# A two-layer decoder trunk: the third strip of each feed-forward part takes four of its eight pairs of row tiles in seven products

## The chip, the cores and the metric

The kernel runs on one core of a Trainium2 chip. The metric is the device time of one launch in microseconds (us). TensorE (PE) multiplies, with its weight loads shown as PEld; VectorE (DVE) and ScalarE (ACT) do the elementwise work; GpSimd (POOL) and SyncE (SP) mainly start transfers.

## The reference, cut to what matters

```python
def swiglu(x, w_gate, w_up, w_down):
    return (jax.nn.silu(x @ w_gate) * (x @ w_up)) @ w_down

for layer in range(DEPTH):                       # DEPTH = 2
    xn = rms_norm(x, norm_mix[layer])
    x = x + mixer(xn)                            # mLSTM + SSD in layer 0, block attention in layer 1
    x = x + swiglu(rms_norm(x, norm_ffn[layer]), *ffn_params[layer])
return rms_norm(x, final_norm)
```

There are 256 tokens, 2048 features and 5632 hidden columns, all in float32. The weights are float32 too, and each is read from memory once.

## The kernel before, in words

**One product is three multiplications.** Each float32 operand is split into a high part, rounded for TensorE, and a low part, the remainder. A product of two operands is then high x high + high x low + low x high, lines 484 to 486 in `add`, each a matmul of 128x128 by 128x512. The weights are split on the fly: ScalarE casts the loaded tile `raw` to `wh` (line 450) and VectorE subtracts to get `wl` (line 452). `raw`, `wh` and `wl` have three buffers each, and `raw` a fourth, `rawx`, in every fourth turn.

**A strip.** The feed-forward has 11 strips of 512 hidden columns. A strip takes the same 512 columns of the gate and of the up weights and runs through the 16 row tiles of 128 features in 8 steps of two tiles (a pair). With two halves of 128 tokens (t) and two outputs (gate and up) a step is a 2x2 by 2x2 block product. It is done in one of two ways, and `plan` says in which order the two ways come:

- P, an ordinary step: eight products, 24 matmuls, into the four banks of `acc_f`. The elementwise work for it is two casts and two subtractions of 128x1024.
- S, a seven-product step (Strassen's scheme in Winograd's form): 21 matmuls, into `acc_f` and the four banks of `acc_e`. It needs four sums of the weight tiles (`sums`, lines 459, 460 and 462, VectorE), which are cast and split like weights, three weight tiles in one 128x1536 piece, and four sums of the activations (`sf`, lines 315 to 318, split into `skx` or `skh`). These are kept in `kt.sums`, so that later strips take them from there.

`PLAN_X` is `PSPSPSPP`, `PLAN_X4` is `PSPSSPSP`. In both the S steps take the pairs 1, 3, 5 in this order, and in `PLAN_X4` also pair 7. The activations' sums of the pairs 1, 3 and 5 are made when the activations are turned; those of pair 7 are made by `sums_of` (line 326, with `xg` from line 331) at step 3 of the strip that uses them, and lie in `skh`, which has three buffers and is shared with the sums of the hidden activations.

**After the last S step** of a strip the banks `acc_e` are drained: ScalarE copies one (line 530), VectorE adds the others (lines 531, 532 and 535). After the last step VectorE adds `acc_f` to that (line 1067, once for each token half). The next strip's `acc_f` takes the same banks, so its first matmul waits for the first instruction of line 1067. Then come the silu (line 1070, ScalarE) and the product with the up half (line 1071, VectorE), which give `h`. For all but the last strip of a part `h` is copied by a transfer of GpSimd's queue to `hr` (line 1074) and turned by TensorE (line 282) one strip later into the `ha` or `hb` blocks (line 225). It is the end of the held stretch (from the first S step to the last) at which that turning may come.

**A part.** The strips are grouped in parts of 4, 4 and 3. After the strips of a part `add_blocks` multiplies their hidden activations by the down weights, in two blocks of the same kind of steps, with `PSPSPSPP` for parts of four strips and with `PSPSPP` (first block) for parts of three, where the S steps take the pairs 1 and 3. Names: `x1..` and `x3..` are the normed activations of the two layers, `ha` and `hb` the hidden ones, `acc_f`/`acc_e` the accumulators, `pre` the drained sums. In the prediction the strips of a part are counted from one: the third strip is `i == 2`.

**What sets the order.** The program is written step by step; a scheduler then orders each engine's instructions by its own model of time and by the priorities given with `tc.high_priority`. Every engine executes its list in order, so what stands behind a waiting instruction waits too.

The lines around the change are these:

## Time and profile before

| | |
|---|---|
| time, median of 3 runs | 2545.25 us (2544.47 to 2546.2) |
| the profiled execution | 2544.58 us, span 2542.8 us |
| TensorE busy | 2529.4 us, 99% |
| weight loads busy | 2118.3 us, 83% |
| VectorE busy | 2227.9 us, 88% |
| ScalarE busy | 1483.9 us, 58% |

Matmuls are pipelined: the profile gives some 390 ns for one of 128x512, while the next one starts earlier than that, so a busy TensorE says little on how fast it goes. What one costs is read from the distance of starts, and from the length of a stretch with a known count. The same holds for VectorE on a smaller scale: its instructions are shown a little longer than the distance to the next one. The time axis starts with the span. The first feed-forward begins with the strip at 761 us, the second with the one at 1837 us.

### The profile page before, as it was taken

What the parts mean: (1) busy time and instruction counts of PE and PEld (TensorE: products, weight loads), DVE (VectorE), ACT (ScalarE), POOL (GpSimd) and SP (SyncE); (2) the same over time, 40 slices, a digit from 0 to 9 for tenths busy, and PEclk for the clock granted to TensorE, in tenths of its full rate; (3) what the DMA queues carried; (4) which work ended last, traced back from release to release, by engine and by line L of the source; (5) the groups of instructions that cost most, each with busy time, mean ns of one, the idle gap of its engine ahead of it and who ended that gap; (6) DMA issues with size and microseconds to landing.
All of it is one profiled execution on the core that took longest, in us unless ns stands there. A gap on an engine that the chain in (4) does not pass through costs nothing.

```text
span 2542.8 us, 32518 instructions
## 1 busy us (share of the span) xinstructions
PE 2529.4 (99%) x12099; PEld 2118.3 (83%) x12099; DVE 2227.9 (88%) x2839; ACT 1483.9 (58%) x1968; POOL 48.5 (2%) x97
## 2 busy tenths in 40 slices
PE   9999999999999999999999999999999999999998
PEld 8888888888888888888888888888888888888887
DVE  5775788898989999999999986767999999999998
ACT  6465565566656655555455665666565555555564
POOL 1000000000000000000000000000000000000000
PEclk9999999999999999999999999999999999999999
DMA  8565575565565657565666656554556566656664
GB/s 289 174 214 180 170 227 171 177 209 188 191 218 178 224 175 231 192 222 187 218 206 208 198 175 231 165 167 146 199 191 208 200 204 215 214 198 197 227 200 166
DMA packets 256383, 505.40 MB, mean 199 GB/s; under 512 B 15976, under 2 KB 16128, under 8 KB 255712
## 3 DMA queue, kind: packets, MB, share of 16 engines
q1 hardware_dynamic: 249952, 483.20, 58.4%
q0 software_dynamic: 4976, 17.43, 1.8%
q10 hardware_dynamic: 1296, 2.69, 0.3%
q8 instruction: 95, 1.56, 0.2%
q14 instruction: 64, 0.52, 0.1%
HBM read 492.66 MB, written 2.14 MB: 195 GB/s over the span
## 4 chain that ended last, share of the span: by engine, by line
PE 95%; DVE 2%; DMA 1%; issue 1%; ACT 0%; POOL 0%; SPq 0%; POOLq 0%; DVEq 0%; ACTq 0%
PE acc_f L484 18%; PE acc_f L486 18%; PE acc_f L485 18%; PE acc_w L393 11%; PE acc_w L397 6%; PE acc_e L484 4%; PE acc_e L485 4%; PE acc_e L486 4%; PE acc_a L424 2%; PE acc_a L423 2%; PE acc_a L422 2%; PE p_tr L284 1%; DMA raw<-in_l_w_o 1%; PE p_y L919 1%; DVE wl L452 0%
## 5 line engine op out<-in xcount | busy, mean ns | idle before, releaser
L450 ACT CAST wh<-raw 128x1024 fp32r<-128x1024 f32 (+1 forms) x563 | 623.0, 1147 | 387.0 <-PE acc_f L486 313.8
L452 DVE TENSOR_TENSOR wl<-raw,wh 128x1024 fp32r<-128x1024 f32 (+1 forms) x563 | 740.8, 1338 | 84.8 <-ACT wh L450 81.4
L484 PE MATMUL acc_f<-wh,x 128*128 128x512 f32 x1086 | 424.8, 391 | 0.0
L486 PE MATMUL acc_f<-wh,x 128*128 128x512 f32 x1086 | 423.0, 389 | 0.0
L485 PE MATMUL acc_f<-wl,x 128*128 128x512 f32 x1086 | 422.7, 389 | 0.0
L450 ACT CAST wh<-sums 128x1024 fp32r<-128x1024 f32 x250 | 256.6, 1051 | 277.6 <-PE acc_f L486 135.0
L379 DVE TENSOR_TENSOR wl<-raw,wh 128x1024 fp32r<-128x1024 f32 x223 | 269.9, 1222 | 115.7 <-ACT wh L378 113.8
L378 ACT CAST wh<-raw 128x1024 fp32r<-128x1024 f32 x223 | 230.7, 1048 | 183.9 <-PE acc_w L393 94.7
L452 DVE TENSOR_TENSOR wl<-sums,wh 128x1024 fp32r<-128x1024 f32 x250 | 298.5, 1219 | 12.3 <-ACT wh L450 11.8
L393 PE MATMUL acc_w<-xa,wh 128*128 128x512 f32 x768 | 264.6, 395 | 1.2 <-DVE xa L227 1.2
L484 PEld LDWEIGHTS acc_f<-wh,x 128*128 128x128 f32 x1086 | 203.9, 188 | 43.0 <-DVE pre L1067 1.4
L486 PEld LDWEIGHTS acc_f<-wh,x 128*128 128x128 f32 x1086 | 203.9, 188 | 42.6
L485 PEld LDWEIGHTS acc_f<-wl,x 128*128 128x128 f32 x1086 | 203.9, 188 | 41.8
L397 PE MATMUL acc_w<-xa,wl 128*128 128x256 f32 x768 | 208.1, 281 | 0.5 <-DVE wl L379 0.5
L393 PE MATMUL acc_w<-x,wh 128*128 128x512 f32 x512 | 182.2, 399 | 0.0
L393 PEld LDWEIGHTS acc_w<-xa,wh 128*128 128x128 f32 x768 | 143.8, 188 | 31.7 <-ACT wh L371 1.5
L459 DVE TENSOR_TENSOR sums<-raw 128x1024 f32<-128x1024 f32 x125 | 152.4, 1219 | 7.0 <-DMA raw<-in_l_w_out 1.9
L397 PEld LDWEIGHTS acc_w<-xa,wl 128*128 128x128 f32 x768 | 142.0, 189 | 2.1 <-DVE wl L379 0.8
L397 PE MATMUL acc_w<-x,wl 128*128 128x256 f32 x512 | 143.3, 280 | 0.0
L393 PEld LDWEIGHTS acc_w<-x,wh 128*128 128x128 f32 x512 | 96.2, 188 | 20.5 <-DVE rsrc L430 0.4
L484 PE MATMUL acc_e<-wh,skx 128*128 128x512 f32 x261 | 101.7, 391 | 0.0
L486 PE MATMUL acc_e<-wh,skx 128*128 128x512 f32 x261 | 101.6, 389 | 0.0
(364 smaller groups left out, 4678.6 us busy)
## 6 DMA issues: line engine op xcount, KB each, us to landing
raw<-in_l_w_in SPq DMA_DIRECT2D x191, 512.0 KB, 3.8
raw<-in_l_ffn_gate SPq DMA_DIRECT2D x176, 512.0 KB, 4.0
raw<-in_l_ffn_up SPq DMA_DIRECT2D x176, 512.0 KB, 4.9
raw<-in_l_ffn_down SPq DMA_DIRECT2D x176, 512.0 KB, 5.1
raw<-in_l_w_qkv SPq DMA_DIRECT2D x96, 512.0 KB, 4.6
raw<-in_l_w_out SPq DMA_DIRECT2D x64, 512.0 KB, 4.9
raw<-in_l_w_o SPq DMA_DIRECT2D x32, 512.0 KB, 4.7
hr<-h POOLq DMA_DIRECT2D x32, 256.0 KB, 3.2
```

Of the source, the lines that this page charges most:

```text
L378: nc.scalar.copy(wh[:, ks, :], raw[:, ks, :])
L379: turn["low"] = nc.vector.tensor_sub(wl[:, ks, :], raw[:, ks, :], wh[:, ks, :].bitcast(F32))
L393: return nc.tensor.matmul(banks[f], wh[:, kk, f * P:(f + 1) * P], kt.both(k0 + kk), start=k0 + kk == 0, stop=False, skip_group_check=True)
L397: nc.tensor.matmul(banks[f][:, :T], wl[:, kk, f * P:(f + 1) * P], kt.parts(k0 + kk)[0], start=False, stop=k0 + kk == nk - 1, skip_group_ch ...
L422: nc.tensor.matmul(banks[t], xh[:, ts], wh[:, kk, :], start=k0 + kk == 0, stop=False)
L423: nc.tensor.matmul(banks[t], xh[:, ts], wl[:, kk, :], start=False, stop=False)
L450: nc.scalar.copy(h[:, c, :], of[:, c, :])
L452: nc.vector.tensor_sub(l[:, c, :], of[:, c, :], h[:, c, :].bitcast(F32))
L459: nc.vector.tensor_sub(sums[:, 0:2, :], raw[:, 2:4, :], raw[:, 3:0:-2, :])
L484: nc.tensor.matmul(dst, ah, bh, start=start, stop=False)
L485: nc.tensor.matmul(dst, ah, bl, start=False, stop=False)
L486: nc.tensor.matmul(dst, al, bh, start=False, stop=stop)
```

## The change

`PLAN_X4` is now also the plan of the third strip of every part, with the pairs 1, 3, 5 and 7. Only the second strip computes the activations' sums of pair 7; they stay in `kt.sums` for the third.

```diff
         def hidden(hT, i, s, plan, copied):
             more = plan == PLAN_X4
             _, pre, both, joined = block(((wg_, s * STRIP), (wu_, s * STRIP)), xt, 0, KD, plan, pairs=(1, 3, 5, 7) if more else None,
-                                         ahead=((3, sums_of, xt, 7, False),) if more else ())
+                                         ahead=((3, sums_of, xt, 7, False),) if more and i == 1 else ())
...
-                hidden(hT, i, first + i, PLAN_X4 if i == 1 else PLAN_X if first + i else PLAN_LATE, i < n - 1)
+                hidden(hT, i, first + i, PLAN_X4 if i in (1, 2) else PLAN_X if first + i else PLAN_LATE, i < n - 1)
```

Six strips are touched (three parts in each of two layers). In the built program TensorE has 18 matmuls fewer; VectorE has six instructions more of each of the lines 459, 460 and 462, six more `wl` pieces of 128x1536 and twelve more of `wl<-sums`, and twelve fewer of `wl<-raw` of 128x1024; ScalarE has the casts that belong to them. The counts of GpSimd's and SyncE's instructions stay.

**VectorE at the end of the third strip of the first part.** `wl<-raw` of 128x1024 are the weights of ordinary steps, lines 531, 532 and 535 drain `acc_e`, and line 1067 frees the banks that the next strip begins with. Before:

```order
L452 TENSOR_TENSOR wl<-raw,wh 128x1024 x3
L531 TENSOR_TENSOR pre<-pre,acc_e 128x512
L452 TENSOR_TENSOR wl<-raw,wh 128x1024
L532 TENSOR_TENSOR pre<-pre,acc_e 128x512
L452 TENSOR_TENSOR wl<-raw,wh 128x1024
L535 TENSOR_TENSOR pre<-pre,acc_e 128x2x512
L452 TENSOR_TENSOR wl<-raw,wh 128x1024
L459 TENSOR_TENSOR sums<-raw 128x1024
L452 TENSOR_TENSOR wl<-raw,wh 128x1536
L460 TENSOR_TENSOR sums<-raw,sums 128x512
L1067 TENSOR_TENSOR pre<-pre,acc_f 128x1024
```

And with the change, from the last ordinary step's weights on:

```order
L452 TENSOR_TENSOR wl<-raw,wh 128x1024 x2
L1071 SCALAR_TENSOR_TENSOR h<-pre,r_7062,h 128x512
L452 TENSOR_TENSOR wl<-raw,wh 128x1024
L531 TENSOR_TENSOR pre<-pre,acc_e 128x512
L452 TENSOR_TENSOR wl<-raw,wh 128x1024
L532 TENSOR_TENSOR pre<-pre,acc_e 128x512
L459 TENSOR_TENSOR sums<-raw 128x1024
L535 TENSOR_TENSOR pre<-pre,acc_e 128x2x512
L460 TENSOR_TENSOR sums<-raw,sums 128x512
L1067 TENSOR_TENSOR pre<-pre,acc_f 128x1024 x2
```

Before, two ordinary steps follow the last S step, and their weights stand between the drains; now one follows, and the second `h` of the strip before stands in this stretch too.

**TensorE where the fourth strip of the first part begins**, with what it waits for in brackets. `p_tr<-ident_r,hr` turns the hidden activations of the second strip, `x_6962` is the first block of activations. With the change:

```order
L486 MATMUL acc_f<-wh,x_7183 128x512
L282 MATMUL p_tr<-ident_r,hr 128x128 [waits DMASW5_49,DVE_49]
L282 MATMUL p_tr<-ident_r,hr 128x128 [waits DMASW6_49]
L282 MATMUL p_tr<-ident_r,hr 128x128
L282 MATMUL p_tr<-ident_r,hr 128x128 [waits DVE_49,PE_49]
L282 MATMUL p_tr<-ident_r,hr 128x128 x4
L484 MATMUL acc_e<-wh,x_6962 128x512 [waits Activation_49]
L484 MATMUL acc_e<-wh,skx 128x512 [waits Activation_49]
L484 MATMUL acc_f<-wh,x_6962 128x512 [waits DVE_49]
```

The turning now stands behind the third strip's last step, where before that step came behind it, and two matmuls of the fourth strip's first S step stand ahead of its first `acc_f` one.

**VectorE in the first down block of the parts with three strips** (layer 0's is shown). `skh<-sf` is the last piece of the first strip's sums, `ha_11872` the second strip's hidden activations. Before, `skh<-sf` stood in the third strip, ahead of the last S step's weights:

```order
L462 TENSOR_TENSOR sums<-raw,sums 128x512
L1071 SCALAR_TENSOR_TENSOR h<-pre,r_7062,h 128x512
L225 TENSOR_TENSOR skh<-sf,skh 128x4x128
L452 TENSOR_TENSOR wl<-sums,wh 128x1024
L452 TENSOR_TENSOR wl<-raw,wh 128x1024 x3
L531 TENSOR_TENSOR pre<-pre,acc_e 128x512
```

With the change it stands behind the end of the strip:

```order
L1067 TENSOR_TENSOR pre<-pre,acc_f 128x1024 x2
L452 TENSOR_TENSOR wl<-raw,wh 128x1536
L462 TENSOR_TENSOR sums<-raw,sums 128x512
L452 TENSOR_TENSOR wl<-sums,wh 128x1024
L459 TENSOR_TENSOR sums<-raw 128x1024
L452 TENSOR_TENSOR wl<-sums,wh 128x1024
L452 TENSOR_TENSOR wl<-raw,wh 128x1024 x2
L460 TENSOR_TENSOR sums<-raw,sums 128x512
L225 TENSOR_TENSOR skh<-sf,skh 128x4x128
L462 TENSOR_TENSOR sums<-raw,sums 128x512
L225 TENSOR_TENSOR ha_11872<-p_tr,ha_11872 128x2x256
L225 TENSOR_TENSOR ha_11872<-xg,ha_11872 128x2x256
```

Both `skh` and the first `ha_11872` are operands of TensorE in this block: in its list the first `skh` low part comes 38th among the matmuls that follow the wait for line 1067, the first `ha_11872` low part 42nd.

## The prediction

> **What bounds the kernel now.** I read the page first, then who TensorE waits for, then the length of stretches with a known count of matmuls.

> ```profile
> PE 2529.4 (99%) x12099; PEld 2118.3 (83%) x12099; DVE 2227.9 (88%) x2839; ACT 1483.9 (58%) x1968; POOL 48.5 (2%) x97
> PEclk9999999999999999999999999999999999999999
> PE 95%; DVE 2%; DMA 1%; issue 1%; ACT 0%; POOL 0%; SPq 0%; POOLq 0%; DVEq 0%; ACTq 0%
> ```

> TensorE is 95% of the chain that ended last, and its clock is never lowered. VectorE at 88% is close behind. TensorE's waits, listed for the weight loads, are tiny:

> ```profile
> PEld acc_e L484 <- DVE ha L225: 1.6, 6, 0.4
> PEld acc_f L484 <- DVE pre L1067: 1.4, 6, 0.3
> ```

> So six waits for line 1067 cost 1.4 us in the whole run. Next, busy time by stretch: a down block without waits, then the third strip of the first part, the third strip of a three-strip part and the down block behind it (length, TensorE, weight loads, VectorE, ScalarE, GpSimd, clock, transfers):

> ```profile
> 974.32:1015.79 41.47, 41.47 (x184) 34.35 (x183) 37.66 (x36) 21.18 (x20) 0.00 (x0) 1.00 0.63 204
> 847.18:889.39 42.21, 42.21 (x192) 34.87 (x191) 41.76 (x45) 25.24 (x29) 1.08 (x2) 1.00 0.66 226
> 1351.01:1393.23 42.22, 42.22 (x191) 34.86 (x191) 41.76 (x45) 25.24 (x29) 1.07 (x2) 1.00 0.68 225
> 1393.23:1426.04 32.81, 32.81 (x147) 26.53 (x146) 29.52 (x34) 18.50 (x21) 0.00 (x0) 1.00 0.56 179
> ```

> The first row is five ordinary and three seven-product steps, 5 x 24 + 3 x 21 = 183 matmuls, in 41.47 us: one costs 0.2266 us. But in the third strip VectorE is busy 41.76 of 42.21 us, with three seven-product steps. The change puts a fourth one exactly there. TensorE bounds the kernel by a hair, and the question is what VectorE does with more work in a stretch that it already fills.

> **What is saved.** Six third strips lose three matmuls each: 18 x 0.2266 = 4.1 us. This is TensorE's time and lies on the path. It is also nearly all that there is to gain, since the waits above are so small. About 0.2% (5.1 us) is what a measurement of this kernel can tell from no change, so even the whole saving would lie within it.

> **What VectorE pays.** Its costs come from the distance of starts at the end of the second strip, which has the new plan already:

> ```profile
> 837.30 2.36 DVE L452 TENSOR_TENSOR wl<-raw,wh 128x1024 fp32r<-128x1024 f32 x2 [1.18 <-ACT wh L450]
> 839.57 1.22 DVE L459 TENSOR_TENSOR sums<-raw 128x1024 f32<-128x1024 f32 x1
> 840.71 0.68 DVE L531 TENSOR_TENSOR pre<-pre,acc_e 128x512 f32<-128x512 f32 x1
> 841.31 1.22 DVE L452 TENSOR_TENSOR wl<-raw,wh 128x1024 fp32r<-128x1024 f32 x1
> 842.44 0.68 DVE L532 TENSOR_TENSOR pre<-pre,acc_e 128x512 f32<-128x512 f32 x1
> 843.04 1.22 DVE L452 TENSOR_TENSOR wl<-raw,wh 128x1024 fp32r<-128x1024 f32 x1
> 844.18 1.21 DVE L535 TENSOR_TENSOR pre<-pre,acc_e 128x1024 f32<-128x1024 f32 x1
> 845.31 0.68 DVE L460 TENSOR_TENSOR sums<-raw,sums 128x512 f32<-128x512 f32 x1
> 845.91 2.34 DVE L1067 TENSOR_TENSOR pre<-pre,acc_f 128x1024 f32<-128x1024 f32 x2
> ```

> An instruction of 1024 takes 1.14 us to the next start, one of 512 takes 0.60. The third strip gives the other sizes:

> ```profile
> 854.05 2.36 DVE L452 TENSOR_TENSOR wl<-raw,wh 128x1024 fp32r<-128x1024 f32 x2
> 856.33 0.68 DVE L460 TENSOR_TENSOR sums<-raw,sums 128x512 f32<-128x512 f32 x1
> 856.93 1.75 DVE L452 TENSOR_TENSOR wl<-raw,wh 128x1536 fp32r<-128x1536 f32 x1
> 858.60 0.68 DVE L462 TENSOR_TENSOR sums<-raw,sums 128x512 f32<-128x512 f32 x1
> 859.21 0.68 DVE L225 TENSOR_TENSOR ha<-p_tr,ha 128x512 fp32r<-128x512 f32 x1
> 860.40 0.28 DVE L315 TENSOR_TENSOR sf<-xg 128x128 f32<-128x128 f32 x1
> 860.61 0.28 DVE L316 TENSOR_TENSOR sf<-xg 128x128 f32<-128x128 f32 x1
> 861.34 0.75 DVE L1071 SCALAR_TENSOR_TENSOR h<-pre,r,h 128x512 f32<-128x512 f32 x1
> 862.02 2.36 DVE L452 TENSOR_TENSOR wl<-sums,wh 128x1024 fp32r<-128x1024 f32 x2
> 864.29 2.35 DVE L452 TENSOR_TENSOR wl<-raw,wh 128x1024 fp32r<-128x1024 f32 x2
> ```

> That is 1.67 us for 1536, 0.20 for an `sf`, 0.67 for line 1071, 2.27 for two of 1024. A seven-product step costs VectorE 1.14 + 0.60 + 0.60 + 1.67 + 2.27 = 6.28 us while TensorE spends 21 x 0.2266 = 4.76; an ordinary one 2.27 us against 5.44. The change adds 6.28 - 2.27 = 4.0 us of VectorE's work to a strip and takes 0.7 us of TensorE's time away; that the sums of pair 7 are not made again only spares adding more. ScalarE, at 25.24 of 42.21 us, has room.

> **The third strip's end.** With the new order VectorE's list is as before up to 859.21. Behind that I add up, word for word along the list, to the first line 1067. The two seven-product steps in a row come first: line 459 and four pieces of 512 1.14 + 2.40, `sf`, `wl<-sums`, `sf` 2.67, the second step's `wl` 1.67 + 2.27, an ordinary step 2.27, together 12.42. Then the last seven-product step with one line 1071 and two `sf` in it: 1.14 + 1.67 + 0.60 + 1.14 + 0.60 + 1.07 + 1.14 = 7.36. Then the ordinary step's weights 2.27, line 1071 0.67, and the drains with the next weights 1.14 + 0.60 + 1.14 + 0.60 + 1.14 + 1.13 + 0.60 = 6.35. The sum is 29.07 us, so line 1067 starts at 888.28, and at the 1.21 us of line 535's row, which has its size, ends at 889.49. Inside the strip I find the weights ready before TensorE needs them. The closest are the three-tile weights of the second adjoining step: 859.21 + 1.14 + 2.40 + 2.67 + 1.75 = 867.2, wanted after 90 matmuls at 847.18 + 90 x 0.2266 = 867.6. ScalarE's casts come in time by its room.

> When does TensorE come there? The same place at the end of the second strip:

> ```profile
> 846.17 0.80 PE L282 MATMUL p_tr<-ident_r,hr 128*128 128x128 f32 x8
> 846.81 0.46 PE L484 MATMUL acc_e<-wh,x 128*128 128x512 f32 x1
> 847.18 0.50 PE L484 MATMUL acc_f<-wh,x 128*128 128x512 f32 x1
> ```

> Eight turns take 0.64 us; without a wait the `acc_f` matmul would have started at 846.81 + 0.23 = 847.04, so the wait was 0.14. With the change the third strip has 180 matmuls, one of them already done at 847.18: 847.18 + 179 x 0.2266 + 0.64 = 888.38, and two matmuls moved ahead bring 888.83. Line 1067 is seen 0.06 us after its end (847.12 to 847.18), at 889.55: a wait of 0.72 us that the third strip does not have now. Six times that is 4.3 us. Its bounds: 0 if VectorE keeps up after all (no gain, since there is no wait to lose), 2.1 if it loses another 1.4 (the second rival). Behind the waiting matmul the whole next strip is queued, so every bit of it is time; but ScalarE and VectorE get on meanwhile, and the next strip, an ordinary one, lets VectorE recover, so I count nothing there.

> **The three-strip parts.** There the down block follows, and VectorE's late work is an operand. Shifted by 1351.01 - 847.18 = 503.83, line 1067 starts at 1392.11 and TensorE goes on at 1393.38. VectorE reaches the end of the first `ha` piece after 2.26 + 1.67 + 0.60 + 1.14 + 1.14 + 1.14 + 2.27 + 0.60 + 0.60 + 0.60 + 0.68 = 12.70 us, at 1404.81. TensorE wants it after 41 matmuls, at 1393.38 + 9.29 = 1402.67: a wait of 2.2 us, with what it waits for `skh` on the way in it. Later, around the last sums, my adding up finds 0.3 us more. Today's block has a wait of its own: 32.81 - 138 x 0.2266 - about 0.8 for its eight turns = 0.7 us. The difference is 1.7 us, twice in the run 3.4 us. Bounds: - 0.7 (today's wait goes too) to 4 us each, the upper one if the turns of the last strip's `h`, which stand behind, come late too.

> **The sum.** - 4.1 + 4.3 + 3.4 = + 3.6 us on this execution's 2544.58, or 2548.2. It lies 0.67 us below the median of the runs, so the median should come to 2548.8, 0.14% above before: no difference that can be told.

> **The rivals.**

> *The whole saving stays.* The scheduler's model had all these instructions before it, and every wait above is one to two us in a chain of 29 us; if VectorE gains 3% anywhere, the waits shrink to nothing. Then - 4.1 us: 2541.2. For it speaks that the second strip runs with the same plan and 0.14 us of wait; against it that the second strip starts with VectorE well ahead and the third does not.

> *VectorE waits for a load in the two adjoining seven-product steps (slower).* By the adding up above, line 459 wants its load at 859.21. The load into that buffer is issued here, for the up half:

> ```profile
> 854.37 0.47 SPq L443 DMA_DIRECT2D raw<-in_l_ffn_up  x1
> ```

> Now, with another load 2.5 us behind it, these two landed after (shortest, median, longest) the first of these rows, and the four halves of loads at 839 to 846, without one so close, after the second:

> ```profile
> DMA to landing us min/median/max: 5.4/5.8/6.2
> DMA to landing us min/median/max: 3.6/4.0/4.5
> ```

> It lands at 858.9 if alone and at 860.6 if not. With the change the next load waits for a buffer that is free only at 859.2, so it should be alone, with 0.3 us to spare. If it is late by 1.4 us, nothing in the chain takes that up: 6 x 1.4 = 8.4 us more, 2557.2.

> *The copies of h come late.* By the same adding up the third strip's second line 1071 ends at 882.0, and TensorE turns its copy at 887.74. GpSimd's instruction takes 0.54 us, and the copy lands after:

> ```profile
> L1074 POOL DMA_DIRECT2D hr<-h x32: 537/537/603, 811.7 to 2452.6; - x32
> DMA to landing us min/median/max: 2.2/3.2/6.3
> ```

> At the median it is there at 885.7, at the longest at 888.8. Then turns and two matmuls end at 889.9 instead of 888.83, 0.4 us behind line 1067: 6 x 0.4 = 2.4 us more, 2551.2. [...] The trace's spread of 2.2 to 6.3 us fits a hindrance of some kind but does not say which. [...]

> *The sums are not kept.* If the third strip computed pair 7's sums again, VectorE would have 0.60 + 4 x 0.20 + 0.60 = 2.0 us more per strip, 12 us in all, 2560.8; against it, the order has no such instructions.

> **How the numbers follow.** My forecast 0.50, the whole saving 0.15, the late load 0.20, the late copies 0.12, sums not kept 0.03. The forecast's own range, with its waits between half and one and a half, is 2545 to 2553. Slower by over 0.2% (above 2550.3): all of the late load and the last rival, most of the late copies, and about a seventh of the forecast, 0.20 + 0.03 + 0.08 + 0.07 = 0.38. Faster by over 0.2% (below 2540.2) needs the whole saving and another 1 us: 0.04. Within: 0.58. The range leaves out the top half of the late load and a part of the whole saving: 2541.5 to 2556.

> **What would show it.** Right: 18 matmuls fewer, the wait for line 1067 at the starts after third strips at 0.5 to 1 us instead of none, `skh` and `ha` behind line 1067 waited for by TensorE in both three-strip down blocks, some 2 us more there, third strips with VectorE busy throughout. Wrong: third strips shorter by 0.7 us with no wait behind them; VectorE idle on line 459 for a transfer in the two adjoining steps; TensorE waiting for `hr`; or waits anywhere else.

## The result and the profile after

The changed kernel takes 2559.19 us (median of 6 runs, 2557.81 to 2562.59), the kernel before in runs beside it 2544.76 us (6 runs, 2544.29 to 2546.2). The ratio is 1.0058, with a 95% interval of 1.0045 to 1.0071: 14.4 us slower. The forecast was 3.6 us slower, and its range ended at 2556. The profiled execution has a span of 2557.7 us, 14.9 more than before.

The page of the changed kernel, TensorE's clock and the chain that ended last:

```profile
PE 2535.0 (99%) x12081; PEld 2116.2 (83%) x12081; DVE 2250.2 (88%) x2863; ACT 1491.4 (58%) x1974; POOL 49.0 (2%) x97
PEclk9999999999999999999999999999999999999999
PE 84%; DVE 9%; DMA 2%; issue 2%; ACT 1%; SPq 0%; POOL 0%; POOLq 0%; ACTq 0%; DVEq 0%
```

The 18 matmuls are gone. TensorE's share of the chain fell from 95% to 84%, and VectorE's rose from 2% to 9%. The shares of busy time do not show it: they are as before. TensorE's waits, by its weight loads (us in total, times, longest):

```profile
PEld acc_f L486 <- DVE skh L225: 4.3, 2, 2.2
PEld acc_e L484 <- DVE ha L225: 3.8, 6, 1.1
PEld acc_f L484 <- DVE pre L1067: 3.7, 12, 0.6
PEld p_tr L282 <- DMA hr<-h: 3.6, 6, 1.1
PEld acc_e L484 <- DVE hb L225: 2.8, 5, 1.7
PEld acc_e L484 <- ACT wh L450: 2.8, 12, 0.4
PEld p_tr L284 <- DVE h L1071: 2.2, 8, 0.4
...
PEld acc_f L484 <- ACT wh L450: 2.1, 1, 2.1
```

Before, `ha` had 1.6 us, `hb` 1.3 and line 1067 1.4, and the other rows here had at most 0.3 or did not stand in the list. Now these three have 3.8, 2.8 and 3.7 us, and the others come on top. By stretch (length, TensorE, weight loads, VectorE, ScalarE, GpSimd, clock, transfers): two third strips, then the first down blocks of the two three-strip parts:

```profile
846.33:890.01 43.68, 42.40 (x190) 34.49 (x190) 42.51 (x46) 25.97 (x29) 1.07 (x2) 1.00 0.65 218
1353.03:1396.29 43.26, 42.33 (x190) 34.47 (x190) 42.59 (x46) 26.17 (x30) 1.08 (x2) 1.00 0.66 217
1396.29:1432.13 35.84, 34.06 (x144) 27.42 (x145) 33.63 (x38) 18.49 (x22) 0.00 (x0) 0.95 0.52 176
2477.63:2517.51 39.88, 36.38 (x146) 28.54 (x146) 34.07 (x39) 18.15 (x21) 0.00 (x0) 0.91 0.58 186
```

The third strips are longer than before, 43.68 and 43.26 us for 42.2, with fewer matmuls. The block at 1396 takes 35.84 us where it took 32.81, and the last one 39.88 where it took 32.34, as this row of before has it:

```profile
2468.98:2501.32 32.34, 32.34 (x148) 26.61 (x146) 28.86 (x35) 18.07 (x20) 0.00 (x0) 1.00 0.62 197
```

The mean clock of the two blocks is 0.95 and 0.91: the clock was lowered, which the page's slices of 64 us hide.

To see where the time went, I cut the span and compare with the same cuts before (us, profiled executions). A part is counted here from the first `acc_f` matmul of its second strip to the same place of the next part; the first three-strip part ends with its down blocks, the second with the span:

| | four-strip parts (4) | three-strip parts (2, with the end) | the rest |
|---|---|---|---|
| the change | +5.0 | +10.5 | -0.6 |

### The profile page after: what moved, and what is told of

Its sections match the earlier page's. It is cut to its first block, busy times and chain, and to the rows that moved or that the text cites. A ratio compares the mean times of both kernels' runs of the same rounds, so it can differ in the third digit from the quotient of the medians.

```text
span 2557.7 us, 32523 instructions
## 1 busy us (share of the span) xinstructions
PE 2535.0 (99%) x12081; PEld 2116.2 (83%) x12081; DVE 2250.2 (88%) x2863; ACT 1491.4 (58%) x1974; POOL 49.0 (2%) x97
## 4 chain that ended last, share of the span: by engine, by line
PE 84%; DVE 9%; DMA 2%; issue 2%; ACT 1%; SPq 0%; POOL 0%; POOLq 0%; ACTq 0%; DVEq 0%
PE acc_f L484 15%; PE acc_f L486 15%; PE acc_f L485 15%; PE acc_w L393 11%; PE acc_w L397 6%; DVE wl L452 4%; PE acc_e L484 4%; PE acc_e L486 4%; PE acc_e L485 4%; PE acc_a L424 2%; PE acc_a L423 2%; PE acc_a L422 2%; DVE sums L459 1%; ACT wh L450 1%; DMA raw<-in_l_ffn_down 1%
## 5 line engine op out<-in xcount | busy, mean ns | idle before, releaser
L450 ACT CAST wh<-raw 128x1024 fp32r<-128x1024 f32 (+1 forms) x557 | 619.4, 1152 | 342.3 <-PE acc_f L486 279.6
L452 DVE TENSOR_TENSOR wl<-raw,wh 128x1024 fp32r<-128x1024 f32 (+1 forms) x557 | 736.2, 1344 | 75.0 <-ACT wh L450 71.7
L450 ACT CAST wh<-sums 128x1024 fp32r<-128x1024 f32 x262 | 270.1, 1051 | 331.2 <-PE acc_f L486 142.9
L484 PE MATMUL acc_f<-wh,x 128*128 128x512 f32 x1050 | 410.6, 391 | 0.2
L486 PE MATMUL acc_f<-wh,x 128*128 128x512 f32 x1050 | 409.0, 390 | 0.0
L485 PE MATMUL acc_f<-wl,x 128*128 128x512 f32 x1050 | 408.6, 389 | 0.0
L452 DVE TENSOR_TENSOR wl<-sums,wh 128x1024 fp32r<-128x1024 f32 x262 | 313.5, 1219 | 8.6 <-ACT wh L450 7.7
L484 PEld LDWEIGHTS acc_f<-wh,x 128*128 128x128 f32 x1050 | 197.1, 188 | 43.0 <-DVE pre L1067 2.7
L486 PEld LDWEIGHTS acc_f<-wh,x 128*128 128x128 f32 x1050 | 197.1, 188 | 41.1
L485 PEld LDWEIGHTS acc_f<-wl,x 128*128 128x128 f32 x1050 | 197.1, 188 | 40.4
L459 DVE TENSOR_TENSOR sums<-raw 128x1024 f32<-128x1024 f32 x131 | 159.6, 1218 | 10.2 <-DMA raw<-in_l_ffn_down 4.9
L484 PE MATMUL acc_f<-wh,hb 128*128 128x512 f32 (+1 forms) x260 | 101.3, 390 | 1.8 <-ACT wh L450 1.7
L486 PE MATMUL acc_e<-wh,skx 128*128 128x512 f32 x261 | 101.6, 389 | 0.0
```

Of the source, the lines that this page charges most:

```text
L450: nc.scalar.copy(h[:, c, :], of[:, c, :])
L452: nc.vector.tensor_sub(l[:, c, :], of[:, c, :], h[:, c, :].bitcast(F32))
L459: nc.vector.tensor_sub(sums[:, 0:2, :], raw[:, 2:4, :], raw[:, 3:0:-2, :])
L484: nc.tensor.matmul(dst, ah, bh, start=start, stop=False)
L485: nc.tensor.matmul(dst, ah, bl, start=False, stop=False)
L486: nc.tensor.matmul(dst, al, bh, start=False, stop=stop)
```

## The first down block of a three-strip part

VectorE of the changed kernel from line 1067 on (start, us):

```profile
1395.02 2.35 DVE L1067 TENSOR_TENSOR pre<-pre,acc_f 128x1024 f32<-128x1024 f32 x2
1397.28 1.75 DVE L452 TENSOR_TENSOR wl<-raw,wh 128x1536 fp32r<-128x1536 f32 x1
...
1403.15 2.36 DVE L452 TENSOR_TENSOR wl<-raw,wh 128x1024 fp32r<-128x1024 f32 x2
1405.43 0.68 DVE L460 TENSOR_TENSOR sums<-raw,sums 128x512 f32<-128x512 f32 x1
1406.03 0.68 DVE L225 TENSOR_TENSOR skh<-sf,skh 128x512 fp32r<-128x512 f32 x1
1406.63 0.68 DVE L462 TENSOR_TENSOR sums<-raw,sums 128x512 f32<-128x512 f32 x1
1407.24 0.68 DVE L225 TENSOR_TENSOR ha<-p_tr,ha 128x512 fp32r<-128x512 f32 x1
```

From line 1067 to the end of the first `ha` piece are 12.90 us; the adding up in the prediction said 12.70. TensorE at that moment:

```profile
1404.59 0.40 PE L485 MATMUL acc_f<-wl,ha 128*128 128x512 f32 x1
1406.77 0.65 PE L486 MATMUL acc_f<-wh,skh 128*128 128x512 f32 x1 [1.78 <-DVE skh L225]
1407.21 0.63 PE L486 MATMUL acc_e<-wh,skh 128*128 128x512 f32 x1
```

The two starts are 2.18 us apart, and the waits row gives 4.3 us for two of them: the wait of 2.2 us that was forecast. But behind it the next start comes after 0.44 and then 0.43 us, not 0.23. The slow stretches of the changed kernel begin at 1406.96, 2488.99 and 2502.64 us and last 3.41 us each; their beginnings lie 317 and 4 times 3.413 us apart, so I cut the span in steps of that length. The first two rows lie beside this wait, the last two beside the longest wait (1.64 us from start to start) of the four-strip parts (length, TensorE busy, clock, transfers):

```profile
1403.55:1406.96 3.41, 1.63 (x8) 1.00 0.75 220
1406.96:1410.38 3.42, 3.42 (x9) 0.50 1.00 377
2280.77:2284.18 3.41, 2.16 (x10) 1.00 0.01 5
2284.18:2287.60 3.42, 3.42 (x16) 1.00 0.05 10
```

TensorE ran at half its clock for exactly one such stretch after the first wait, and not after the second. It happens three times in the changed kernel, always in three-strip parts, and before not once from 4.69 to 2537.37 us of its span (mean clock 1.00). 19 matmuls took 0.427 instead of 0.227 us, 3.8 us, and those at the stretches' edges were slowed in part (0.40 us at 2488.90). All told it is some 4.8 us: eight matmuls of 0.427 us fill a stretch that would hold fifteen of 0.227, so each of the three cost 1.6 us. In the last part a second wait of 2.1 us follows 13 us behind the first (the row of line 450 with one wait above: the casts are late), with its own slow stretch.

## The experiments

Theory from these rows: VectorE has too much to do, or does it in the wrong order, at the end of the third strip; what the down block needs comes late, and a long enough wait halves the clock. Rivals came with each test. All times are medians, beside the kernel before on the same chip (2544.0 to 2545.4 us). The losses by part, as in the table above, come from each profiled execution. The pieces of code show only what differs, often a part of a line.

| run | time, us | ratio to before, interval | four-strip | three-strip | rest |
|---|---|---|---|---|---|
| e1_four | 2555.31 | 1.0043 (1.0030, 1.0056) | +4.8 | -0.4 | +5.9 |
| e2_three | 2556.56 | 1.0044 (1.0031, 1.0056) | -0.1 | +8.8 | +3.2 |
| e3_prio | 2562.41 | 1.0069 (1.0056, 1.0081) | +4.4 | +12.6 | +1.0 |
| e10_prio2 | 2556.09 | 1.0049 (1.0036, 1.0061) | +6.5 | +5.2 | -0.4 |
| e11_allprio | 2567.90 | 1.0093 (1.0079, 1.0107) | +13.8 | +11.3 | -1.2 |
| e7_less | 2554.58 | 1.0034 (1.0022, 1.0046) | +2.0 | +9.5 | -0.3 |
| e13_less_prio | 2550.14 | 1.0024 (1.0014, 1.0033) | +2.2 | +2.2 | +0.3 |
| e14_double | 2552.59 | 1.0032 (1.0019, 1.0044) | +1.7 | +5.2 | -0.1 |
| e9_pool | 2580.51 | 1.0138 (1.0125, 1.0152) | +19.4 | +17.4 | +1.8 |
| e16_alt | 2557.80 | 1.0053 (1.0039, 1.0067) | +7.0 | -0.1 | +7.4 |
| e6_early | 2587.71 | 1.0170 (1.0156, 1.0184) | +29.1 | +16.7 | -0.7 |
| e4_again | 2599.86 | 1.0219 (1.0203, 1.0235) | +35.2 | +18.0 | +0.3 |
| e5_swap | 2588.63 | 1.0169 (1.0155, 1.0183) | +32.0 | +16.1 | +0.5 |
| e12_fill | 2559.88 | 1.0065 (1.0051, 1.0079) | +9.0 | +8.7 | +0.9 |
| e8_fill | 2585.02 | 1.0155 (1.0141, 1.0169) | +18.4 | +8.9 | +10.1 |
| e15_pad | 2573.75 | 1.0115 (1.0101, 1.0129) | +15.4 | +3.2 | +9.9 |

In the rows quoted from the experiments a line's number can be one to four higher than the change's. Single executions scatter. The four-strip parts have one and the same order in the change, e3_prio, e10_prio2 and e12_fill, and lost 5.0, 4.4, 6.5 and 9.0 us, so a difference of a few microseconds in one column alone says little.

### Which parts lose

e1_four, the new plan in four-strip parts alone; e2_three, with `n == 3`:

```diff
-PLAN_X4 if i in (1, 2) else
+PLAN_X4 if i == 1 or i == 2 and n == 4 else
```

> The new plan for the third strip of the parts with four strips alone (four of the six strips). Theory (the loss sits mainly in the three-strip parts: the down block behind the third strip waits 2 us for the first strip's sums, and TensorE's clock is halved behind that wait): these four parts cost 0.5 to 1.8 us each in the profile of the change, 5.1 us together, so about 2550, and no clock of 0.5 inside the span. Rival (every third strip loses about the same, since VectorE is full in each): two thirds of the 14.4 us, about 2554.

> The new plan for the third strip of the two three-strip parts alone. Theory: these two parts cost 3.8 and 6.7 us in the profile of the change, so about 2555, with the weight-load waits for skh (line 225) of some 2 us each and two or three stretches of 3.4 us at half clock. Rival (every third strip alike): one third of 14.4 us, about 2549.5.

The two add up to 21.8 us, more than the change. By time alone e1_four went to the rival. The time of e2_three is close to the theory's. By part the theory holds for both: each kind loses about what it loses in the change, 4.8 and 8.8 us for 5.0 and 10.5, and the untouched kind nothing. The surplus of e1_four is in "the rest", at the passage from the attention layer to the second feed-forward, where no line differs (of e2_three's 3.2 us 1.6 are lost there). Before, the change and e1_four there:

```profile
1793.33:1881.07 87.74, 87.50 (x403) 72.58 (x402) 84.27 (x109) 56.10 (x79) 0.69 (x1) 1.00 0.62 207
```

```profile
1799.39:1887.14 87.75, 87.46 (x402) 72.57 (x402) 84.12 (x109) 56.70 (x79) 0.69 (x1) 1.00 0.61 206
```

```profile
1795.41:1889.76 94.35, 90.23 (x403) 74.58 (x402) 84.70 (x109) 56.21 (x79) 1.12 (x1) 0.96 0.58 191
```

The same work takes 6.6 us longer. In e1_four the scheduler put two casts of the feed-forward's first weights about 10 us later in ScalarE's list than before, and TensorE waits 3.9 us in one piece:

```profile
PEld p_tr L284 <- ACT skx L225: 3.9, 1, 3.9
```

Behind this wait the clock is at half for 6.83 us (its mean from 1840 to 1850 us is 0.66), which the theory for this run had excluded. So an edit in one place changed the order in another, hundreds of microseconds on. The change itself does not suffer from it (87.75 us).

### The order in VectorE's queue

e3_prio moves the turnings of the three-strip parts forward, e10_prio2 also lines 1070 and 1071 (the silu and the product that make `h`) of their last strip, e11_allprio both in all strips. The lines shown are those of e10_prio2:

```diff
-        with tc.high_priority(offset=1200 if first else 0):
+        with tc.high_priority(offset=1200 if first or kt.name in ("ha8", "hb8") else 0):
...
+                with tc.high_priority(offset=0 if copied or hT.name not in ("ha8", "hb8") else 1200):
```

> The change as it is, but the turning of hidden activations in the three-strip parts is given a higher priority in the scheduler, so that the first strip's sums and the second strip's hidden activations stand earlier in VectorE's list; no work is added or taken away. Theory (late operands and the clock behind them): the waits for skh go, the clock stays full, and 6 to 8 us of the 10.5 us of these two parts come back, 2551 to 2553. Rival (VectorE's total work is the bound there, in whatever order): the waits move to other operands and the time stays within 2 us of 2559.

> As the run that moved the turnings of the three-strip parts forward, and with the two products that make h of their last strip moved forward too (they were what came late there). Theory (it is the order in VectorE's queue: what the down block waits for stands behind splits of weights that are wanted later): the 10.5 us lost in the three-strip parts fall to under 4, no half clock there, 2549 to 2553 us. Rival (VectorE has too much to do at that place whatever comes first, so that another instruction is late by as much): 2556 us or more, with another name in the waits.

> The changed kernel, with the turnings and the products that make h moved forward in all strips of the feed-forward parts. Theory of the order: the waits of the four-strip parts (5 us) shrink as well as those of the three-strip parts, 2541 to 2549 us. Rival (the amount): the splits of weights are late in their place, TensorE waits for wh and wl inside the strips, 2556 to 2575 us.

e3_prio lost no less than the change (more than the rival's bound too), and the theory of the order alone fell. The waits for `skh` left the list; another came:

```profile
PEld p_tr L284 <- DVE h L1071: 8.4, 10, 3.9
```

The turnings now stood ahead of line 1071, TensorE had to wait up to 3.9 us for `h`, and the clock was at half for 6.83 us in each of the two parts (its mean over the execution is 0.996, for 0.997 in the change). With that moved too (e10_prio2) the loss in the three-strip parts is halved, 10.5 to 5.2 us, and no stretch there is at half clock (0.999 over the execution, as before). That is not under 4 as the theory asked, and the time, 2556.1, is at the rival's edge; its interval overlaps that of the change. With everything forward (e11_allprio) the splits of weights are what comes late, as the rival had it:

```profile
PEld acc_e L485 <- DVE wl L452: 21.1, 30, 1.6
PEld acc_e L484 <- ACT wh L450: 11.4, 17, 2.0
```

Whatever is put first, something else is late: the order chooses who waits.

### The amount of VectorE's work

e7_less leaves out three subtractions in the third strip (the sums of weights of its last S step are not formed, and the raw weights are split in their place), e13_less_prio adds e10_prio2's order, e14_double adds three to the kernel before, e9_pool gives three to GpSimd:

```diff
+            if summed == "less":
+                return parts(raw, (slice(0, 3),)) + parts(raw, (slice(0, 2), slice(2, 4)))
...
+            for _ in range(2 if summed == "twice" else 1):
...
+            eng = nc.gpsimd if summed == "pool" else nc.vector
```

> The changed kernel, and for the last of the four seven-product row tiles of the third strip the three VectorE subtractions that build the sums of weights are left out (the raw weights are split in their place), so 1.2 + 0.7 + 0.7 = 2.6 us of VectorE less in each third strip, with the same matmuls. Theory (VectorE's work alone is late): the waits of 2.2 us in the three-strip parts go, and the half clock with them; 2545 to 2549 us. Rival (the waits are set by the order, by the bank that the turning shares or by loads, not by how much VectorE has to do): little changes, 2555 to 2560 us.

> The two partial remedies together: in the third strip the three subtractions for the sums of weights of the last seven-product tile are left out (2.6 us of VectorE; the raw weights are split in their place), and the turnings and the two products for h of the last strip of the three-strip parts are moved forward in the order. Theory (VectorE's amount in the third strip makes the waits, and its order only says which instruction is the late one): with both, the three-strip parts lose under 2 us instead of 10.5, the four-strip parts 1.6 us as with the first alone, no half clock; 2544 to 2548 us. Rival (something besides VectorE, as the banks or the loads, holds the down block): 2551 us or more.

> The kernel before the change, with the three subtractions for the sums of weights of one seven-product tile of the third strip done twice (same values): 2.6 us of VectorE more in each third strip, no matmul moved. Theory (VectorE's work in that strip is what costs): waits appear in TensorE at the same places as with the change, which adds 4.3 us of VectorE: 2547 to 2554 us. Rival (VectorE has slack there, and the fourth seven-product tile hurts through its matmuls, their banks or their place): within 2 us of before.

> The changed kernel, with the three subtractions for the sums of weights of the last seven-product row tile of the third strip on GpSimd instead of VectorE, 2.6 us of VectorE less in each third strip. Theory (VectorE's work is late and GpSimd has time: it is busy 2%): 2545 to 2550 us. Rival (GpSimd takes much longer for them than VectorE's 2.6 us, or slows VectorE while it works, so that TensorE waits for those weights): no better than 2557 us, up to 2580.

e7_less cured the four-strip parts (5.0 to 2.0 us) but hardly the three-strip ones: the time set free was filled with splits for later, and a split became the late one, so that half clock came here too (the first down block of the first three-strip part takes 36.99 us at a mean clock of 0.95). By time, 2554.6 us, it lies at the rival's edge.

```profile
PEld acc_e L487 <- DVE wl L452: 5.2, 6, 2.2
```

With both remedies the loss went from 14.4 to 5.4 us, below the rival's bound but above the theory's 2544 to 2548. The down block of the first three-strip part there:

```profile
1396.15:1429.21 33.06, 33.00 (x146) 26.22 (x146) 31.12 (x36) 18.49 (x22) 0.00 (x0) 1.00 0.62 199
```

33.06 us against 35.84, at full clock, 0.25 us from the 32.81 of before. The other direction, e14_double, is the plainest: no matmul is moved, and 2.6 us of VectorE more in each third strip make the kernel 7.9 us slower, as the theory said. The place is the same, the late operands are not: in the first down blocks of the two three-strip parts TensorE waits for splits (`wl`, 2.0 and 1.3 us) and for `ha` or `hb` (1.0 us each). The clock is 1.00 in the first of these blocks:

```profile
1394.30:1429.52 35.22, 33.35 (x148) 26.39 (x146) 31.57 (x36) 18.70 (x21) 0.00 (x0) 1.00 0.53 174
```

GpSimd is no way out (e9_pool), as the rival had it. Its three pieces take 3.3, 1.6 and 2.7 us, 7.6 together where VectorE takes 2.6, and ScalarE's casts wait for them (20.5 us in six waits). VectorE's pieces are longer there as well: in each of the six strips its split of 128x1536 beside GpSimd's second and third piece took 2.84 or 2.85 us, where others took 1.75; no run shows why.

```profile
L460 POOL TENSOR_TENSOR sums<-raw 128x1024 f32<-128x1024 f32 x6 | 19.8, 3304 | 328.9 <-DMA raw<-in_l_ffn_up 165.2 <-DVE wl L452 163.7
...
L463 POOL TENSOR_TENSOR sums<-raw,sums 128x512 f32<-128x512 f32 x6 | 16.1, 2687 | 0.5
L461 POOL TENSOR_TENSOR sums<-raw,sums 128x512 f32<-128x512 f32 x6 | 9.7, 1619 | 0.5
```

### Its neighbours and its place

e16_alt gives the plan to the second and the fourth strip of four-strip parts, and to the second alone in three-strip parts, e6_early moves its S steps forward, e4_again makes pair 7's sums anew in the third strip, e5_swap has the plan in the third strip alone:

```diff
+PLAN_X4 if i == 1 or i == 3 and n == 4 else
...
+PLAN_X4E = "PSSPSSPP"
...
+ahead=((3, sums_of, xt, 7, False),) if more else ())
...
+PLAN_X4 if i == 2 else
```

> The seven-product strips apart: second and fourth strip in the four-strip parts, only the second in the three-strip parts, with the second strip's sums kept for the fourth. Theory of the amount, with VectorE catching up in the plain strip between: 0 to 0.7 us less in each of the four parts, 2541 to 2546 us. Rival (a seven-product strip straight ahead of a down block costs there, one before it or not): 2 to 3 us more in each of the four parts, 2550 to 2558 us.

> The changed kernel, with the third strip's order PSSPSSPP instead of PSPSSPSP (S: seven products): its last seven-product tile is one tile earlier and two plain ones follow. Theory (what is late is VectorE's drains and turning at the strip's end): the waits of 2.2 us in the three-strip parts shrink below 1 us and the half clock goes, 2548 to 2554 us. Rival (VectorE cannot keep up with seven-product tiles side by side: two pairs of them need 2 x 6.8 us of VectorE for 2 x 4.8 us of TensorE): TensorE waits for weights inside the third strips, 2558 to 2575 us.

> The change, but the third strip computes the activations' sums of pair 7 again (one subtraction pass of 512, four of 128, one split: 2.0 us of VectorE per strip, TensorE the same). Theory: VectorE has no slack between the adjoining seven-product steps and line 1067, so nearly all of it comes on top, 6 x 2.0 = 12 us, 2567 to 2573. Rival (VectorE has slack, only late operands behind the strip count): under 3 us more, 2559 to 2562.

> Only the third strip has four seven-product tiles, the second strip has three as the others; the third strip makes its own sums of activations. As many matmuls as before the change. Theory A (the strip straight ahead of the down block is the wrong place, since VectorE's drains and splits of that strip end late): the three-strip parts keep their loss of 8 to 10 us, the four-strip parts lose nothing against before, 2552 to 2556 us, with waits of 2 us and half clock in the first down block of the three-strip parts. Theory B (two such strips in a row are the trouble, VectorE enters the third strip already behind): one alone costs nothing, 2543 to 2547 us, no wait over 1 us there.

e16_alt went to the rival: with a plain strip between the two, the four parts still lose 7.0 us, 1.8 each, about half of it in the fourth strip and half in the down block behind it. A strip with four S steps straight ahead of a down block costs there. (Another 7.4 us are the passage of e1_four again.) e6_early missed the theory by far, and by another way than its rival's: TensorE waits for the drains of `acc_e`, which the next S step's banks and the turning now need at once.

```profile
PEld acc_e L485 <- ACT pre L531: 13.2, 6, 2.5
PEld p_tr L283 <- DVE pre L532: 7.2, 6, 2.0
```

e4_again and e5_swap were meant as tests of the sums and of the neighbours, and both came out beyond every expectation, so they test neither cleanly. The sums asked for within the third strip come late, by up to 5.3 us in e4_again and 2.9 in e5_swap, and stretches at half clock follow in every part: the mean clock of the two executions is 0.994 and 0.992, for 0.999 before, and in e4_again 0.94 in the 52.78 us of the second part's third strip. First e4_again, then e5_swap:

```profile
PEld acc_f L484 <- ACT skh L225: 29.3, 6, 5.3
```

```profile
PEld acc_f L484 <- ACT skh L225: 14.3, 6, 2.9
```

### The clock, and a tile's place

e12_fill puts eight matmuls by zeros a little ahead of the one that waits for `skh` (the first lines below); e8_fill was the same with a tile of zeros of its own; e15_pad has the kernel before with such a tile, unused:

```diff
+            for _ in range(fill):
+                nc.tensor.matmul(dst[:64], ident_r[0:64, 64:P], bh[0:64], start=False, stop=False)
...
+    none = cst.tile([P, 32], F32, name="none")
+    nc.gpsimd.memset(none, 0.0)
```

> The changed kernel, with eight matmuls by a tile of zeros (they add nothing to the result) put in TensorE's order into the wait of 2.2 us in the first down block of each three-strip part: 8 x 0.227 = 1.8 us. Theory (TensorE waiting for about 2.1 us is what halves the clock): the wait shrinks to some 0.4 us, the half clock after it goes (7 matmuls in the one part, 5 in the other at 0.427 instead of 0.227 us, so 2.4 us), and what follows from the slow stretch in the last part, 2553 to 2557 us. Rival (the clock is lowered for another reason, or the wait is not shortened but the eight come on top): half clock stays, 2559 to 2563 us.

> The changed kernel, with eight matmuls by zeros (a corner of the identity, nothing is added to the result, and no tile is added) in TensorE's order ahead of the matmul that waits 2.2 us in the first down block of each three-strip part: 8 x 0.227 = 1.8 us. Theory (a TensorE idle for about 2 us within one stretch of 3.413 us gets half clock in the next): the wait shrinks to some 0.4 us, no half clock follows it, 12 matmuls at 0.227 instead of 0.427 us or 2.4 us less; the later wait for the casts in the last part may keep its own; 2555 to 2558 us. Rival (the clock goes down for another reason, or the fills come on top): half clock stays at both places, 2559 to 2563 us.

> The kernel before the change, with one unused tile of 128 bytes per partition kept through the kernel, so that all that is placed after it lies 128 bytes further. Theory (the first run with fills took 25 us more than the changed kernel, all of it in matmuls of 232 instead of 227 ns in the strips, because of that tile's place): 2563 to 2573 us. Rival (the zeros themselves did it): 2543 to 2547 us.

In e12_fill every engine has the changed kernel's order but for the 16 fills. While TensorE works on the fills VectorE catches up, and the gap before `skh` is gone in both parts: 0.23 us from start to start instead of 2.18. No half clock follows this matmul: the first part's whole block has 1.00 where it had 0.95. In that part, the fills, the matmul by `skh` with the one ahead of it, and the whole block (as the rows by stretch above):

```profile
1406.78 2.08 PE L487 MATMUL acc_f<-wh,ident_r 64*64 64x512 f32 x8
1410.50 0.39 PE L485 MATMUL acc_f<-wl,ha 128*128 128x512 f32 x1
1410.73 0.39 PE L488 MATMUL acc_f<-wh,skh 128*128 128x512 f32 x1
```

```profile
1399.96:1434.79 34.83, 34.74 (x152) 26.98 (x153) 33.65 (x38) 18.17 (x21) 0.00 (x0) 1.00 0.55 179
```

The block takes 34.83 us instead of 35.84 although 2.0 us of fills are in it. The later gap for casts in the last part is still 2.12 us, so the first slow stretch did not cause it, and it keeps its own half clock (TensorE is busy for 1.66 of the 3.41 us ahead of it, for 1.70 in the change; the mean clock of the execution is 0.998, for 0.999 before). So a wait of this size, 2.18 us from start to start, can lower the clock, as the theory said. The time did not fall as expected and lies in the rival's range: the profiled execution gains 1.8 us in the three-strip parts and loses 4.0 in the four-strip ones, whose order is untouched, and the median is that of the change within the scatter.

e8_fill's 25 us above the change come from the tile's place: e15_pad, without any fill, is 29 us slower than before, a little more than expected. The down block and the strip behind it, the same 183 matmuls each, in e15_pad:

```profile
984.23:1025.72 41.49, 41.49 (x185) 1.00 0.61 203
1025.72:1068.25 42.53, 42.53 (x184) 1.00 0.59 198
```

No wait, full clock, and 1.05 us more in the strip, where before both took 41.48.

## Why the prediction was wrong

**What held.** The saving, 18 matmuls. VectorE's price, 4.0 us a strip (the page has VectorE busy 22.3 us longer, 3.7 a strip), and the adding up along its list: 12.70 against 12.90 us to the first `ha`, and two waits of 2.2 us, as worked out, for what it named. The profiled execution lost 14.9 us where 3.6 were forecast. Of the 11.3 us between, 7.2 lie in the first down blocks of the three-strip parts (10.6 for 3.4) and 3.5 in those of the four-strip parts (3.5 for nothing).

**"Its clock is never lowered."** This was read off the profile before and carried into a program with longer waits. No term of the sum held a clock. It cost some 4.8 us in three slow stretches. Together with the later wait of 2.1 us for casts, which the adding up did not reach, it makes the two blocks, forecast at + 1.7 us each, lose 3.0 and 7.5. This step failed most. In the changed kernel gaps of 2.18, 2.18 and 2.08 us from start to start, in stretches of 3.41 us with TensorE busy for 1.63, 1.64 and 1.70 us, were each followed by 3.41 us at half clock.

**"The next strip, an ordinary one, lets VectorE recover, so I count nothing there."** That strip did not suffer: it is 0.34 us shorter, by the matmuls moved ahead of it. But behind it the first down blocks of the four four-strip parts lost 3.5 us: TensorE's first `acc_e` matmul waits there for `ha` or `hb` (0.5 to 1.7 us, for 0.4 before), since two of the four banks of `acc_e` are also those that turnings use. e16_alt and e7_less say the same from both sides: these blocks lose 3.5 us as well when a strip with four S steps stands right ahead of them, and 0.6 when the third strip has less to do.

**The wait for line 1067** was oversized: 4.3 us forecast, 3.7 - 1.4 = 2.3 found. VectorE was late, and even 1.3 us more than forecast (888.72 for 888.28, and the strip starts 0.85 us earlier). But TensorE came later too: it had waited inside the strip, where the forecast had looked at the weights alone. In every part the turning at the strip's end waited for `hr` first (0.2 to 1.1 us), and in the first part TensorE had also waited 1.1 us for `ha`, behind a late load:

```profile
859.31 1.22 DVE L459 TENSOR_TENSOR sums<-raw 128x1024 f32<-128x1024 f32 x1 [0.88 <-DMA raw<-in_l_ffn_up]
860.46 0.68 DVE L225 TENSOR_TENSOR ha<-p_tr,ha 128x512 fp32r<-128x512 f32 x1
```

**The rivals.** The late load came true there, and held VectorE for 0.88 us, where it was priced at 1.4 us in every strip. With the 0.85 us by which the strip starts earlier, 859.31 is 860.16 on the forecast's axis, between its two landings of 858.9 and 860.6. The late copies of `h` came true: six waits, 3.6 us, for 2.4 forecast. They were kept as alternatives to the forecast though both add to it, and that is an error of form: at the strip's end the wait for line 1067 and the one for `hr` together came to 5.9 us, where the forecast and this rival together had 6.7. The sum, 3.6 + 2.4 and the 0.9 us of the late load, would have pointed above the number given, but only to some 7 us; the lowered clock and the four-strip down blocks were in no rival.

**What is settled and what is not.** Shown: the loss follows VectorE's work in the third strip (e14_double up, e13_less_prio down; e7_less alone lies lower than the change too, but the two intervals just touch), the order decides which wait is long (e3_prio, e10_prio2, e11_allprio), and a wait of 2.2 us can lower the clock (e12_fill). Not settled: the last 5 us that remain in e13_less_prio (2 of them in the first part, behind late loads), and whether another plan could keep the saving. None of these kernels beats the one before.

## What to carry to other kernels

Price an exchange between two engines in both currencies: here 0.7 us of TensorE was bought with 4.0 us of an engine that had 0.5 us to spare in that strip. When the second engine is full, do not look for the one wait that comes of it; count the surplus and expect it at every place that it serves, wherever the order sends it. Ask of each wait that you forecast whether it may lower the clock, as gaps of 2.1 to 2.2 us did three times here, and compare parts of the program, not totals, since a scheduler may reorder what nobody edited.

## What the runs showed of the hardware

```profile
2280.92:2284.33 3.41, 1.68 (x8) 1.00 0.01 3
2284.33:2287.75 3.42, 3.42 (x16) 1.00 0.05 14
```

So by these runs the border lies about here, and the busy time of one stretch does not settle it. In e2_three the same gap of 2.18 us in the first three-strip part fell across two stretches, with TensorE busy for 2.99 and 2.04 of 3.41 us, and the clock of the next one was 1.00: by this pair it counts as well where a gap falls.

**128 bytes.** An unused tile of 128 bytes per partition, placed ahead of the others, made the matmuls of the strips take 0.232 instead of 0.227 us from start to start (42.53 and 41.48 us for 183), 1.05 us a strip and 29 us over the run. Which operand's address does it was not tried; the down blocks, which take `ha` and not `x`, kept their pace (41.49 us for 183, before 41.47).
